# A 16 KB store of one row of 16 partitions, issued ahead of the first 4 MB store of a DMA-bound kernel

## Chip, cores and metric

One core of a Trainium2 chip. The metric is the device time of one execution in microseconds (us), the median over several executions. Each execution also has a span, the time from the first to the last recorded instruction of the core; the span of this kernel is about 1.6 us shorter than its device time. Fast means within 1.5% of the fastest execution of the same kernel. One core runs, so there is no die to compare.

## The reference

```python
W_adapted = W + scale * (lora_A @ lora_B)                 # 256 x 256
W_norm = np.sqrt(np.sum(W_adapted ** 2, axis=0, keepdims=True) + 1e-8)
W_final = W_adapted / W_norm * m
y = x.reshape(-1, 256) @ W_final                          # x: 16 x 2048 x 256, float32
```

x is 32 MB and y is 32 MB. The weights are small.

## The kernel before

The 32,768 rows are cut into 8 blocks of 4 MB. A block lies in SBUF as 128 partitions with one contiguous row of 32 KB each. There are 5 such buffers. SP issues the loads, and each result is written over its input in the same buffer, so a buffer is loaded, computed in place and stored. ACT copies the products out of PSUM, chunk by chunk (8 chunks of 512 KB per block), and issues the store when a block is complete. The last block is loaded and stored in two halves.

```python
def load_x(n):
    nc.sync.dma_start(
        out=in_sbuf(*parts[n]), in_=in_dram(x_flat, *parts[n])
    ).then_inc(sem(f"load{n}"), 16)

def store_y(n):
    nc.scalar.dma_start(
        out=in_dram(out_flat, *parts[n]), in_=in_sbuf(*parts[n])
    ).then_inc(sem(f"store{n}"), 16)

# ... SP: the first five loads at once, a later one when the store of its buffer has landed
for n in range(len(parts)):
    b = parts[n][0] // CH
    if b >= XBUFS and parts[n][0] % CH == 0:
        nc.sync.wait_ge(sem(f"store{b - XBUFS}"), 16)
    load_x(n)

# ... ACT
for g in range(NCH):                                   # 64 chunks
    b, c = divmod(g, CH)
    nc.scalar.wait_ge(sem("product"), g + 1)
    nc.scalar.copy(
        out=x_bufs[b % XBUFS][:, c * J : (c + 1) * J, :], in_=y_ps[g % 2][:]
    ).then_inc(sem("room"), 1)
    n = part_of[g]
    if g == NCH - 1 or part_of[g + 1] != n:
        nc.scalar.drain().then_inc(sem("done"), 1)
        nc.scalar.wait_ge(sem("done"), n + 1)
        store_y(n)
```

## Time and profile before

| | before |
|---|---|
| median of the timed executions | 163.63 us (163.5 to 163.79, 3 runs) |
| the execution that was profiled | 164.71 us, span 163.2 us |
| load queue q1 / store queue q10 | 49.0% / 47.8% of the 16 DMA engines' span |
| HBM traffic | 33.85 MB read, 33.55 MB written, 413 GB/s over the span |

Lines of the profile's page of the kernel before. The DMA and GB/s lines cut the span into 40 slices (4.08 us each): the first has the busy share of the DMA engines in tenths, the second what they moved. The q lines give packets, megabytes and the share of 16 engines' span.

```profile
span 163.2 us, 1988 instructions
...
DMA  5998998998999999999999999999999999998991
GB/s 201 402 498 386 426 474 385 482 418 265 466 426 426 442 410 466 426 394 482 418 426 442 420 426 458 402 458 410 446 414 454 414 446 422 450 442 377 442 430 60
...
q1 hardware_dynamic: 1440, 33.82, 49.0%
q10 hardware_dynamic: 1474, 33.59, 47.8%
```

The DMA engines are busy at eight tenths or more from the second slice to the last but one, so they bound the kernel. The tenth slice, with 265 GB/s, is the one low point on the way. (A slice holds only some 50 packets of 32 KB, so neighbours differ by some 100 GB/s without meaning.)

The timeline of the kernel before, ACT alone (start, duration, engine, line, operation; in brackets the idle time before it and what ended it):

```profile
23.65 1.93 ACT L219 COPY x_sb<-y_ps 128x1024 f32<-128x1024 f32 x2 [13.20 <-PE y_ps L281]
25.88 1.93 ACT L219 COPY x_sb<-y_ps 128x1024 f32<-128x1024 f32 x2 [0.30 <-PE y_ps L281]
30.26 1.93 ACT L219 COPY x_sb<-y_ps 128x1024 f32<-128x1024 f32 x2 [2.45 <-PE y_ps L281]
32.49 1.93 ACT L219 COPY x_sb<-y_ps 128x1024 f32<-128x1024 f32 x2 [0.30 <-PE y_ps L281]
34.52 0.37 ACTq L128 DMA_DIRECT2D out_dram<-x_sb  x1
```

The first store is issued at 34.52 us, right ahead of the low slice. The trace also holds every single DMA packet (start, duration, bytes, queue). A 32 KB row takes 1.213 us again and again. Between 36.1 and 38.4 us 25 load packets start that take 1.3 to 2.9 us. Adding up what those packets (the ones over 1.3 us) take beyond 1.213 us and dividing by 16 engines gives 1.29 us per engine. (The records do not name a packet's engine; "per engine" is here a sum over packets, or their number, divided by 16. In this trace 16 packets of 16 KB or more are on their way at once for 148 of the 163.2 us.) This sum is called "the stall" below. It is work on packet records, not a view of the profile. A count of bytes checks it: spreading the bytes of each packet evenly over its time, the core moved 413.7 GB/s from 20 to 50 us and 432.6 GB/s from 60 to 110 us, and what is missing in the first stretch is worth 1.3 us. So the stall is lost traffic and not only packets that overlap.

The packet records show a second loss. A store ends with 16 packets of 4 bytes. I take them as one for each engine, so that the last 16 of them tell when each engine was done: 15 engines have written their last byte by 160.3 us, one only at 162.7 us. 42 of the 896 store packets of 32 KB take 1.228 to 1.359 us (median 1.26), the others under that; no two of the 42 overlap by more than 0.01 us, so they fit one engine.

### The profile page before, as it was taken

Reading aid. Unit: us, or ns where it says so; the run is one execution under the profiler, and the core shown is the slowest. Engines: PE = TensorE matmul, PEld = TensorE weight load, DVE = VectorE, ACT = ScalarE, POOL = GpSimd, SP = SyncE. Lnnn points to the kernel's source line nnn. Section 1 sums busy time; section 2 is a strip of 40 time slices with the busy share of each in tenths; the row PEclk is TensorE's granted clock in tenths of the full one; section 3 lists DMA queues with packets and bytes.
Section 4 is the critical chain, followed back from the end, with each engine's and each line's share of the span. In section 5 each row is a group of like instructions: output and inputs, shape, how many; then the busy total and the mean of one; then the engine's idle time right before and its main releaser. Section 6 shows DMA issues by size and latency. Waiting matters only on the chain. (4 is left out here: it accounts for less than half of the span.)

```text
span 163.2 us, 1988 instructions
## 1 busy us (share of the span) xinstructions
PE 105.3 (65%) x786; PEld 85.2 (52%) x786; DVE 47.2 (29%) x44; ACT 63.8 (39%) x67; POOL 62.5 (38%) x39
## 2 busy tenths in 40 slices
PE   1270599789789897898981998619988820892000
PEld 0130577677577775776760867418676610771000
DVE  0429452350532514405230325005051400330000
ACT  3010027548366384473754053900738440062000
POOL 1006381753935738268004940069209003900000
PEclk9999999999999999999998589985899996599755
DMA  5998998998999999999999999999999999998991
GB/s 201 402 498 386 426 474 385 482 418 265 466 426 426 442 410 466 426 394 482 418 426 442 420 426 458 402 458 410 446 414 454 414 446 422 450 442 377 442 430 60
DMA packets 2915, 67.41 MB, mean 413 GB/s; under 512 B 465, under 2 KB 482, under 8 KB 610
## 3 DMA queue, kind: packets, MB, share of 16 engines
q1 hardware_dynamic: 1440, 33.82, 49.0%
q10 hardware_dynamic: 1474, 33.59, 47.8%
q14 instruction: 1, 0.01, 0.0%
HBM read 33.85 MB, written 33.55 MB: 413 GB/s over the span
## 5 line engine op out<-in xcount | busy, mean ns | idle before, releaser
L219 ACT COPY x_sb<-y_ps 128x1024 f32<-128x1024 f32 x64 | 61.9, 1014 | 75.8 <-PE y_ps L281 75.8
L165 POOL CAST xb<-x_sb 128x2048 bf16<-128x2048 f32 x32 | 60.0, 1902 | 79.3 <-DMA x_sb<-in_x_dram 56.0
L281 PE MATMUL y_ps<-w_final,xt 128*128 128x256 bf16 x512 | 64.6, 280 | 12.8 <-PEq L256 12.8
L202 DVE COPY xt<-xt_ps 128x1024 f32<-128x1024 f32 x32 | 38.2, 1221 | 88.1 <-PE xt_ps L267 88.0
L281 PEld LDWEIGHTS y_ps<-w_final,xt 128*128 128x128 bf16 x512 | 48.4, 100 | 28.2 <-issue 19.8
L267 PE MATMUL xt_ps<-identity,xb 128*128 128x128 f32 x264 | 39.1, 309 | 23.1 <-PEq L256 23.1
L267 PEld LDWEIGHTS xt_ps<-identity,xb 128*128 128x128 f32 x264 | 34.9, 161 | 25.8 <-issue 25.6
L198 DVE TENSOR_TENSOR w_final<-wam,rnorm 128x256 bf16<-128x256 f32 x2 | 4.0, 2028 | 0.0
L244 PE MATMUL y_ps<-sq,ones 128*128 128x256 f32 x4 | 2.1, 674 | 1.6 <-DVE sq L187 1.6
L233 PE MATMUL y_ps<-identity,a_nat 128*16 128x128 f32 x2 | 0.6, 397 | 3.6 <-DMA a_nat<-in_lora_A_dram 3.6
L212 ACT ACTIVATE norm<-y_ps,eps_col 128x256 f32<-128x256 f32 x1 | 0.5, 473 | 6.1 <-PE y_ps L244 6.1
L244 PEld LDWEIGHTS y_ps<-sq,ones 128*128 128x128 f32 x4 | 1.2, 323 | 2.3 <-DVE sq L187 2.1
L210 ACT ACT_TABLE_LOAD x1 | 1.3, 1283 | 2.4 <-issue 2.4
L233 PEld LDWEIGHTS y_ps<-identity,a_nat 128*16 128x16 f32 x2 | 0.1, 90 | 3.6 <-issue 3.6
L171 POOL MEMSET xb<- 128x2048 bf16 x1 | 1.8, 1805 | 0.3 <-PE xt_ps L267 0.3
L195 DVE RECIPROCAL rnorm<-norm 128x256 f32<-128x256 f32 x1 | 1.7, 1745 | 0.0
L237 PE MATMUL y_ps<-b_bf,aT 16*128 16x256 bf16 x2 | 0.6, 404 | 1.5 <-DVE aT L180 1.5
L189 DVE COPY m_all<-y_ps 128x256 f32<-128x256 f32 x1 | 0.4, 425 | 3.3 <-PE y_ps L249 3.3
L178 DVE CAST b_bf<-b_nat 16x256 bf16<-16x256 f32 x1 | 0.3, 281 | 3.8 <-DMA b_nat<-in_lora_B_dram 3.8
L249 PE MATMUL y_ps<-m_row,ones 1*128 1x256 f32 x2 | 1.2, 710 | 0.0
L237 PEld LDWEIGHTS y_ps<-b_bf,aT 16*128 16x128 bf16 x2 | 0.1, 106 | 1.9 <-DVE aT L180 1.9
L183 DVE SCALAR_TENSOR_TENSOR wa<-y_ps,w_nat 128x512 f32<-128x512 f32 x1 | 0.7, 692 | 0.8 <-PE y_ps L237 0.8
(13 smaller groups left out, 3.7 us busy)
## 6 DMA issues: line engine op xcount, KB each, us to landing
x_sb<-in_x_dram SPq DMA_DIRECT2D x7, 4096.0 KB, 27.1
out_dram<-x_sb ACTq DMA_DIRECT2D x7, 4096.0 KB, 37.2
x_sb<-in_x_dram SPq DMA_DIRECT2D x2, 2048.0 KB, 29.6
out_dram<-x_sb ACTq DMA_DIRECT2D x2, 2048.0 KB, 20.2
w_nat<-in_W_dram SPq DMA_DIRECT2D x1, 256.0 KB, 2.9
a_nat<-in_lora_A_dram ACTq DMA_DIRECT2D x1, 16.0 KB, 2.6
b_nat<-in_lora_B_dram ACTq DMA_DIRECT2D x1, 16.0 KB, 3.6
m_row<-in_m_dram ACTq DMA_DIRECT2D x1, 1.0 KB
```

What stands on the lines that cost most here:

```text
L165: nc.gpsimd.tensor_copy(out=xb_bufs[p % NXB][:], in_=x_bufs[b % XBUFS][:, 2 * c * J : 2 * (c + 1) * J, :],).then_inc(sem("rounded"), 1)
L171: nc.gpsimd.memset(xb_bufs[NPR % NXB][:], 0.0).then_inc(sem("rounded"), 1)
L183: nc.vector.scalar_tensor_tensor(out=wa[:], in0=ab_ps, scalar=float(scale), in1=w_nat[:], op0=ALU.mult, op1=ALU.add).then_inc(dv, 1)
L195: nc.vector.reciprocal(out=rnorm[:], in_=norm[:]).then_inc(dv, 1)
L198: i = nc.vector.tensor_mul(out=w_final[:, t], in0=wam[:, t], in1=rnorm[:])
L202: nc.vector.tensor_copy(out=xt_bufs[p % NXT][:].rearrange("p r t -> p (r t)").bitcast(FP32), in_=xt_ps[p % 2][:],).then_inc(sem("copied"), 1)
L210: nc.scalar.activation(out=warm[:], in_=eps_col[:], func=AF.Sqrt)
L219: nc.scalar.copy(out=x_bufs[b % XBUFS][:, c * J : (c + 1) * J, :], in_=y_ps[g % 2][:]).then_inc(sem("room"), 1)
L244: i = nc.tensor.matmul(n2_ps, ones[:], sq[:, t, :], start=(t == 0), stop=(t == KC - 1))
L249: nc.tensor.matmul(mb_ps, ones[0:1, :], m_row[:], start=True, stop=True).then_inc(pe, 1)
L267: i = nc.tensor.transpose(xt_ps[p % 2][:, j * P : (j + 1) * P], xb_bufs[p % NXB][:, j, :].bitcast(FP32), identity[:],)
L281: i = nc.tensor.matmul(y_ps[h][:, j, :], xt_bufs[p % NXT][:, r : r + P, t], w_final[:, t, :], start=(t == 0 and (j % (J // 2)) == 0), stop ...
```

## The change

The intent: let the first write of the program be a tiny one, so that whatever the first write costs does not hold up 32 KB rows of loads. After the second chunk, one row of 1 KB of each of 16 partitions goes out, meant as one packet for each DMA engine. The whole block is still stored later, over it.

```diff
         ).then_inc(sem("room"), 1)
+        if g == 1:
+
+            nc.scalar.drain().then_inc(sem("first"), 1)
+            nc.scalar.wait_ge(sem("first"), 1)
+            nc.scalar.dma_start(
+                out=in_dram(out_flat, *parts[0])[0:16, 0:1, :],
+                in_=x_bufs[0][0:16, 0:1, :],
+            ).then_inc(sem("ahead"), 16)
         n = part_of[g]
+        if n == 0 and g == NCH // NBLK - 1:
+            nc.scalar.wait_ge(sem("ahead"), 16)
         if g == NCH - 1 or part_of[g + 1] != n:
```

## The prediction

> **What bounds the kernel now.** The 16 DMA engines. The DMA part of the page has the load queue at 49.0% and the store queue at 47.8% of the engines' span, 158 of 163.2 us; the 40 slices show DMA at 9 nearly throughout. The other engines have room (PE 65%, ACT 39%). In the timeline a 4 MB block is computed in 13.2 us (first store issued at 34.52, second at 47.74), while its load and store take the DMA about 19.4 us. The chain of waits is no use: it covers 2% of the span. The last store is issued at 148.20 us; 15 us of store traffic follow. Time is won only where DMA engines now lose it.
>
> **What they lose.** In the records of single DMA packets a 32 KB row takes 1.213 us. One exception touches all 16 engines: from about 36 to 39.6 us, just after the first store is issued, load packets take 1.3 to 2.9 us. Summed and divided by 16, 1.3 us are lost per engine; the 40 slices show 265 GB/s in the tenth slice, where neighbours have 418 and 466. The first store packet starts 5 us after its issue. No later store brings this. I read it as a one-time cost of the first write to HBM, with loads stuck behind 16 rows of 32 KB.
>
> A second loss is not touched: one engine's store packets take about 1.26 us, and it finishes at 162.7 us, 2.4 us after the others.
>
> **What the change does.** It adds a store of 16 KB (16 partitions, 1 KB each) after the second copy out of PSUM, near 26 us, 9 us before the first whole store. Nothing is removed. Costs: a 1 KB packet takes 0.046 us, so 0.05 us per engine; ACT gives a drain, a wait and an issue of about 0.4 us, in a stretch where it idles 2.45 us before each four copies and where loads alone keep the DMA busy until about 48 us. If the whole store slips by 0.5 us, nothing waits for it. The added wait should be over before the eighth copy.
>
> The first write's cost should then fall on 1 KB per engine. [...] If instead the first write stops the memory for everybody, the 1.3 us move to 27 us.
>
> **Sum.** All avoided: 163.6 - 1.3 + 0.05 = 162.4. Merely moved: 163.7. I give avoidance, wholly or largely, 60%. What is saved counts in full, since DMA is busy to the end.
>
> Predicted 162.8 us, 8 in 10 between 161.9 and 163.9. Faster by over 2%: 0.02; within 2%: 0.96; slower: 0.02.
>
> **What would show it.** Right: the tenth slice over 400 GB/s, no packet over 1.5 us near 36 to 40 us, no slice below 380 near 26 to 31 us, the whole store's first packet within 3 us of its issue. Wrong (moved): an equal dip in the seventh or eighth slice. Wrong (cause is not the first write): the dip stays after the first whole store.
>
> **What would make it wrong.** The stall needs large rows or the first store's many descriptors rather than a first write; the small store completes so late that block 0's store slips by many us; the slow engine becomes slower or recovers (up to 2.4 us either way).

## The result, and the profile after

| | before | after |
|---|---|---|
| median | 163.69 us (163.5 to 163.79, 4 runs) | 163.68 us (163.62 to 163.72, 4 runs) |
| ratio after / before | | 1.000 (95% interval 0.9983 to 1.0017) |
| profiled execution | 164.71 us, span 163.2 | 163.72 us, span 162.1 |

A ratio is the mean time of one kernel's fast runs over that of the other's of the same rounds, so it is not quite the ratio of the medians.

The time did not change. The two profiles differ by 1.1 us in span, but the two profiled executions also differ by 1.0 us in device time. The first trace of the kernel before is therefore the wrong thing to compare with. Run e6 below profiled the unchanged kernel again, in an execution of 163.67 us; it is shown here with the changed kernel.

The page of the changed kernel, the same lines as shown of before, and its line on the new store (KB, us from issue to landing):

```profile
span 162.1 us, 1990 instructions
...
DMA  5999999998999999989999999999989999999992
GB/s 198 392 509 396 388 509 396 392 509 315 461 388 453 453 388 453 453 388 485 412 404 493 398 404 485 404 400 437 485 372 429 449 441 465 404 429 408 441 429 121
...
q1 hardware_dynamic: 1440, 33.82, 49.2%
q10 hardware_dynamic: 1506, 33.61, 48.2%
...
out_dram<-x_sb ACTq DMA_DIRECT2D x1, 16.0 KB, 6.4
```

The page of the unchanged kernel profiled again (run e6):

```profile
span 162.1 us, 1988 instructions
...
DMA  5999999997999999999999999999999999999993
GB/s 202 413 485 396 420 477 396 429 477 283 485 388 420 485 396 429 461 404 437 453 404 461 431 404 477 412 396 445 433 416 445 412 441 489 404 412 425 433 420 137
```

The span is the same to the tenth. The low tenth slice is still there after the change (315 GB/s against 283). The seventh and eighth slice, where the prediction put a moved stall (the small store's packets run in the eighth), are at 396 and 392 in the changed kernel and 396 and 429 in the unchanged one; the difference of 37 is within what neighbours differ by.

The timeline of the changed kernel, ACT alone:

```profile
23.45 1.93 ACT L219 COPY x_sb<-y_ps 128x1024 f32<-128x1024 f32 x2 [11.30 <-PE y_ps L291]
25.48 0.34 ACTq L226 DMA_DIRECT2D out_dram<-x_sb  x1
25.86 1.93 ACT L219 COPY x_sb<-y_ps 128x1024 f32<-128x1024 f32 x2 [0.49 <-PE y_ps L291]
30.06 1.93 ACT L219 COPY x_sb<-y_ps 128x1024 f32<-128x1024 f32 x2 [2.27 <-PE y_ps L291]
32.28 1.93 ACT L219 COPY x_sb<-y_ps 128x1024 f32<-128x1024 f32 x2 [0.30 <-PE y_ps L291]
34.32 0.37 ACTq L128 DMA_DIRECT2D out_dram<-x_sb  x1
```

The same stretch of e6 begins and ends with:

```profile
23.27 1.93 ACT L219 COPY x_sb<-y_ps 128x1024 f32<-128x1024 f32 x2 [12.58 <-PE y_ps L281]
...
34.14 0.37 ACTq L128 DMA_DIRECT2D out_dram<-x_sb  x1
```

The new store costs ACT 0.19 us (0.49 instead of 0.30 before the next pair of copies), and the next wait is shorter by 0.18 us. So issuing it is free.

From the packet records:

| | before, first profile | before again (e6) | after |
|---|---|---|---|
| device time of that execution | 164.71 | 163.67 | 163.72 |
| small store: packets start | | | 28.9 to 30.2 us |
| longest load packet starting from 26 to 31.5 us | 1.264 | 1.213 | 1.222 |
| whole store: issue, first packet | 34.52, 39.59 | 34.14, 39.26 | 34.32, 39.25 |
| stall at the whole store, us per engine | 1.29 | 0.96 | 0.71 |
| last byte of 15 engines / of the last engine | 160.3 / 162.7 | 160.1 / 161.6 | 160.2 / 161.6 |

The small writes pass among the loads without holding up any of them (no load packet over 1.222 us), and the whole store still stalls the loads. The count of bytes from 20 to 50 us agrees: against the same 432.6 GB/s, 0.9 us are missing in e6 (419.2 GB/s) and 0.7 us in the changed kernel (422.0). The longer first profile of before differs from e6 mostly by its slow engine: 1.1 us at its end, against 0.4 us for the mean of the other 15, which is about what its stall is longer (0.33 us).

### The profile page after: what moved, and what is told of

It is laid out like the page before. It is cut to its first block, busy times and chain, and to the rows that moved or that the text cites. A ratio compares the mean times of both kernels' runs of the same rounds, so it can differ in the third digit from the quotient of the medians.

```text
span 162.1 us, 1990 instructions
## 1 busy us (share of the span) xinstructions
PE 103.0 (64%) x786; PEld 83.7 (52%) x786; DVE 45.6 (28%) x44; ACT 63.6 (39%) x67; POOL 62.4 (38%) x39
## 5 line engine op out<-in xcount | busy, mean ns | idle before, releaser
L291 PE MATMUL y_ps<-w_final,xt 128*128 128x256 bf16 x512 | 63.4, 276 | 12.8 <-PEq L266 12.7
L291 PEld LDWEIGHTS y_ps<-w_final,xt 128*128 128x128 bf16 x512 | 47.8, 99 | 27.6 <-issue 19.6
L277 PE MATMUL xt_ps<-identity,xb 128*128 128x128 f32 x264 | 38.0, 303 | 23.8 <-PEq L266 23.8
L277 PEld LDWEIGHTS xt_ps<-identity,xb 128*128 128x128 f32 x264 | 34.0, 158 | 26.4 <-issue 26.2
L198 DVE TENSOR_TENSOR w_final<-wam,rnorm 128x256 bf16<-128x256 f32 x2 | 2.5, 1276 | 0.0
```

Source lines behind the costliest of these rows:

```text
L198: i = nc.vector.tensor_mul(out=w_final[:, t], in0=wam[:, t], in1=rnorm[:])
L277: i = nc.tensor.transpose(xt_ps[p % 2][:, j * P : (j + 1) * P], xb_bufs[p % NXB][:, j, :].bitcast(FP32), identity[:],)
L291: i = nc.tensor.matmul(y_ps[h][:, j, :], xt_bufs[p % NXT][:, r : r + P, t], w_final[:, t, :], start=(t == 0 and (j % (J // 2)) == 0), stop ...
```

## The experiments

Theory A: the stall does not belong to the first write. It comes when long store packets first run beside the loads, so a small store takes nothing away, and 0.71 against 0.96 is chance. Theory B: the small store does shrink the stall, and something else eats the gain. Rivals about the cause of the stall follow run by run. "Early" is always after the second chunk, as in the change.

### e1 and e6: the kernel before again; e2 and e5: the changed kernel again

No edit. e1 and e5 were the first kernel of their job.

> The kernel before, unchanged, profiled again, because the first profile of it came from an execution of 164.71 us while its timed runs have a median of 163.69. Theory A (the small store removed nothing, the two first profiles differ by chance): span about 162.1 us, stall of the loads at the first whole store about 0.7 us per engine, time ratio 1.000. Theory B (the small store halved the stall and something else ate the gain): span about 163.2 us with a stall of about 1.3 us again.

> The changed kernel, unchanged, profiled again. Theory A: time ratio 1.000 within 0.1%, and the stall at the first whole store between 0.7 and 1.3 us per engine, anywhere in the range that the kernel before shows. Theory B: stall again near 0.7 us, below that of the kernel before on this chip. Both: no stall when the small store's packets run near 29 us.

> The changed kernel as the first kernel of a job. Both profiles of the kernel before came from the first execution of a job (164.71 and 164.81 us, span 163.2), both of the changed kernel from later ones or other jobs (163.72 and 163.65, span 162.1). If it is the place in the job that costs 1.1 us, this profile shows a span near 163.2 us and its first time is near 164.7 us; the other times are 163.6 to 163.8. If the kernel before is slower under the profile by itself, this stays at 162.1.

> The kernel before, as the second kernel of a job, to have a trace of an execution as long as its timed ones. If the small store removed nothing: span 162.1 us, stall of the loads at the first whole store 0.7 to 0.9 us per engine as in the two traces of the changed kernel. If the small store does shrink it: 1.1 us or more at the same span.

| run | kernel | median, ratio to before (95%) | profiled execution | stall at the whole store |
|---|---|---|---|---|
| e1 | before | 163.61, 0.999 (0.998 to 1.000) | 164.81, span 163.2 | 1.06 |
| e6 | before | 163.66, 0.999 (0.997 to 1.001) | 163.67, span 162.1 | 0.96 |
| e2 | after | 163.73, 1.001 (0.9995 to 1.0025) | 163.65, span 162.1 | 0.84 |
| e5 | after | 163.85, 1.000 (0.997 to 1.003) | 163.90, span 162.4 | 0.94 |

e1 missed what theory A expected: its profiled execution was again a long one (its other six took 163.49 to 163.78), and its stall of 1.06 us lies between the two theories. Being first in the job is not enough for a long execution, as e5 shows. e1's trace does show where its extra time went. The loads stalled three times more, near 55, 75 and 94 us, by 0.39, 0.56 and 0.52 us per engine; the 16 engines ended 1.5 us later on average than in e6, and the last one 1.1 us later. Why these stalls come in some executions only is not shown. The page of e1 has the first stall in its ninth slice (257); of the later ones only those in slices 19 and 24 (361 and 363) stand out a little:

```profile
span 163.2 us, 1988 instructions
...
GB/s 201 426 474 385 490 410 393 506 257 474 418 426 458 385 401 458 418 434 361 450 434 434 450 363 434 426 458 385 434 458 401 438 434 422 482 409 418 414 434 173
```

e6 gave the trace that was wanted, and its 0.96 us too lies between what was expected if the small store removed nothing (0.7 to 0.9) and if it shrinks the stall (1.1 or more). With 0.71, 0.84 and 0.94 us after and 0.96 before at like times, the stall is not clearly different, and the ratio of the first comparison (0.9983 to 1.0017) allows at most about 0.3 us of gain or loss. Theory B is not excluded for a tenth or two of a microsecond. It is excluded as a halving: e5 has 0.94.

### e3: 128 partitions of 1 KB instead of 16

```diff
-                out=in_dram(out_flat, *parts[0])[0:16, 0:1, :],
-                in_=x_bufs[0][0:16, 0:1, :],
+                out=in_dram(out_flat, *parts[0])[:, 0:1, :],
+                in_=x_bufs[0][:, 0:1, :],
```

> The early store widened from 16 to 128 partitions, 1 KB each: 8 descriptors per engine and every 32 KB row of the block touched once. If the cost belongs to the first touch of each piece of the output or to the first long list of descriptors, the loads are held up near 29 us and the first whole store is free (under 0.2 us). If it belongs to the first long store packets (theory A's reading), nothing near 29 us, and 0.7 to 1.3 us at the whole store as before; time ratio 1.000 to 1.001 (128 KB more are 0.3 us of DMA).

Median 164.82 us, ratio 1.0065 (1.0051 to 1.0079). From 26 to 35 us, while its packets ran, no load packet was held up (0.00 us), and the whole store stalled the loads by 0.92 us. So neither the first touch of every 32 KB row of the block nor a list of 128 descriptors is what costs. The time is up by 1.1 us, more than expected. The profiled execution was its fastest (164.16 us, span 162.5), and its 8 packets of 0.046 us per engine account for 0.4 us; why the other five had spans of 163.2 to 163.5 us is open.

### e4: the first store in two pieces, nothing stored twice

```diff
-                out=in_dram(out_flat, *parts[0])[0:16, 0:1, :],
-                in_=x_bufs[0][0:16, 0:1, :],
+                out=in_dram(out_flat, *parts[0])[:, 0 : 2 * J, :],
+                in_=x_bufs[0][:, 0 : 2 * J, :],
...
+        j0 = 2 * J if n == 0 else 0
-            out=in_dram(out_flat, *parts[n]), in_=in_sbuf(*parts[n])
+            out=in_dram(out_flat, *parts[n])[:, j0:, :], in_=in_sbuf(*parts[n])[:, j0:, :]
```

> No byte is stored twice: block 0 is stored as 8 KB rows of all 128 partitions after the second chunk and as 24 KB rows after the eighth. If the cost comes when long packets of the store queue first meet the loads, the stall moves to about 29 us, perhaps smaller as the packets are a quarter (0.2 to 0.7 us per engine), and the later store of 24 KB rows, for which the queue is by then empty again, shows little or a stall of its own. If it is bound to the first write alone it is at 29 us in full (0.7 to 1.3 us) and nothing later. Time: 163.0 to 163.7 us.

Median 163.74 us, ratio 1.000 (0.9988 to 1.0012). Load packets were held up at three places: 0.29 us from 25 to 28, 0.11 near 33, and 0.17 near 44 us when the rows of 24 KB began, 0.57 us in all. So 8 KB packets, eight per engine, do meet the stall, in a milder form, where 1 KB packets do not. It lost less in all than the 0.96 us of e6, and no time was won. In its profiled execution the last engine ended at 161.5 us as ever.

### e7 and e10: a full 32 KB row per engine in the early store

Its data are the second block as loaded, written to rows that the whole store overwrites; the output is right. e7 takes partitions 0 to 15, e10 every eighth partition.

```diff
             nc.scalar.wait_ge(sem("first"), 1)
+            nc.scalar.wait_ge(sem("load1"), 16)
             nc.scalar.dma_start(
-                out=in_dram(out_flat, *parts[0])[0:16, 0:1, :],
-                in_=x_bufs[0][0:16, 0:1, :],
+                out=in_dram(out_flat, *parts[0])[0:128:8, :, :],     # e7: [0:16, :, :]
+                in_=x_bufs[1][0:128:8, :, :],                        # e7: [0:16, :, :]
```

> The early store of 16 partitions carries a full 32 KB row per engine instead of 1 KB (its data are the loaded second block, written to rows that the whole store overwrites, so the output is right). It adds 512 KB, 1.2 us per engine. If the stall belongs to the first long store packet of the program, 0.5 us or more move to 27 to 31 us and the whole store has under 0.2 us. If it is paid each time the store queue goes from empty to long packets while loads run, both places show it (0.3 us or more early, 0.5 us or more at the whole store). Time 164.8 to 165.5 us.

> The early store of 16 full 32 KB rows again, from every eighth partition instead of sixteen neighbours, because with neighbours the early packets themselves took 1.6 to 4.1 us. If that was crowding on the few SBUF partitions read, the packets now take 1.2 us, the loads near 27 us lose 0.5 to 1.0 us per engine, the whole store loses under 0.2, and the time is 164.6 to 165.3 us. If the early stall was not crowding, it stays at 1.5 us or more and the time at 166.7.

e7: 166.72 us, ratio 1.0158 (1.0111 to 1.0205), over the 165.5 us that were expected. Its 16 packets took 1.6 to 4.1 us each, 1.9 us per engine beyond 1.213, and the loads beside them lost 0.10 us. The whole store, whose packets begin at 37.05 us, stalled the loads by 0.01 us. e10: 164.69 us, ratio 1.0070 (1.0056 to 1.0085). Its 16 packets took 1.213 us each, the loads lost 0.60 us between 27.5 and 29 us, and the whole store 0.00.

The page of e10:

```profile
span 163.0 us, 1991 instructions
...
GB/s 197 414 482 394 418 482 386 386 418 482 386 458 442 386 474 426 402 482 402 434 458 394 452 442 394 482 410 450 386 434 462 450 386 446 458 386 434 426 430 133
```

The tenth slice is at 482 GB/s: no low point where the whole store begins. This is the result that fixes the place of the cost, and e7 agrees with it; each rests on one profiled execution. One long packet per engine beside the loads takes the stall over, though the store queue then moved no data for over 5 us (the last early packet ends at 32.2 us, the next starts at 37.75). It takes the stall over and does not remove it: 0.60 us are lost early instead, and the 512 KB add 1.2 us of traffic. Some of the 0.60 us may belong to the choice of partitions and not to the stall, since in e7, with neighbouring partitions, the loss at that place fell on the early packets themselves and was much larger; no run separates this.

### e8: the store queue made busy with a load

Kernel before, with the fifth load issued by ACT at the second chunk instead of by SP:

```diff
+        if g == 1:
+            nc.scalar.dma_start(
+                out=in_sbuf(*parts[4]), in_=in_dram(x_flat, *parts[4])
+            ).then_inc(sem("load4"), 16)
...
-        load_x(n)
+        if n != 4:
+            load_x(n)
```

> No early store. The fifth load is issued on the store queue, at the second chunk, so that this queue becomes busy with 32 KB packets that are loads; store 0 then follows behind it on a queue that is never empty. If the stall comes from a second queue becoming busy, it appears near 28 us with loads alone (0.5 us or more) and not at store 0. If it comes from writing to HBM, nothing near 28 us and 0.5 us or more when store 0's packets begin. Time 163.0 to 164.2 us.

Median 163.68 us, ratio 1.000 (0.997 to 1.002). The load's 32 KB packets ran on the store queue from 26.3 us, and none of its packets took over 1.225 us. The last packet of that load started at 43.5 us and the store's first at 46.3 us, so the queue did stand without data packets for a moment. Load packets of the other queue that started from 43.3 to 47.6 us lost 0.75 us, and another 0.28 us was lost near 77 us. A second queue becoming busy is not enough; the stall came with the store.

### e9 and e12: writing before the loads run

e9 writes 1 MB of zeros in 8 KB rows at the very start and holds the loads of x until it has landed. e12 stores one 32 KB row per engine after the first load and holds the second load until that has landed. Both drop the early store among loads; the whole store overwrites what they wrote. (Of each edit the wait of ACT for the early store ahead of store 0 is cut.)

```diff
+    nc.vector.memset(x_bufs[0][:, 0 : 2 * J, :], 0.0).then_inc(sem("blank"), 1)     # e9
+    nc.scalar.wait_ge(sem("blank"), 1)
+    nc.scalar.dma_start(
+        out=in_dram(out_flat, *parts[0])[:, 0 : 2 * J, :],
+        in_=x_bufs[0][:, 0 : 2 * J, :],
+    ).then_inc(sem("ahead"), 16)
+    nc.sync.wait_ge(sem("ahead"), 16)
...
```

```diff
+    load_x(0)                                                                       # e12
+    nc.scalar.wait_ge(sem("load0"), 16)
+    nc.scalar.dma_start(
+        out=in_dram(out_flat, *parts[0])[0:128:8, :, :],
+        in_=x_bufs[0][0:128:8, :, :],
+    ).then_inc(sem("ahead"), 16)
+    nc.sync.wait_ge(sem("ahead"), 16)
-    for n in range(len(parts)):
+    for n in range(1, len(parts)):
...
+        if g == 0:
+            nc.scalar.wait_ge(sem("ahead"), 16)
...
```

> No early store among loads. At the very start 1 MB of zeros (8 KB rows of 128 partitions) is written to the first block's rows, and the loads of x wait until it has landed; the whole store overwrites it. If the stall is a cost of the first bulk write of an execution, it is paid there, and the whole store of block 0 holds up the loads by under 0.2 us. If it comes from long stores meeting running loads for the first time, it stays at 0.7 to 0.95 us at the whole store. Time 167 to 171 us in both cases, because the loads start later.

> One 32 KB store packet per engine (every eighth partition) goes out after the first load has landed and before the second load is issued, so no load runs beside it. If what counts is that long store packets meet running loads, these packets take their 1.2 us and the whole store of block 0 still stalls the loads by 0.5 us or more. If the length of the first store packet alone counts, the whole store has under 0.2 us, and the cost shows as longer packets or not at all. Time 168 to 171 us, because the second load starts late.

e9: 169.10 us, ratio 1.0332 (1.0317 to 1.0347). Its early store packets of 8 KB took 0.307 to 0.341 us, a quarter of 1.213 us and a little: no start-up cost is seen in them. The whole store still stalled the loads by 0.77 us. e12: 170.60 us, ratio 1.0406 (1.0353 to 1.0458). Its 16 packets took 2.2 to 2.6 us with nothing beside them, about twice 1.213 us, and the whole store stalled the loads by 1.20 us. So e9's first write pays nothing that shows at its own place. e12's does take longer, though e10's packets from the same partitions took 1.213 us; why is not shown. What was written before the loads ran, short or long, does not spare the whole store the stall. The loads that start right behind these early stores lose 0.62 us (e9) and 0.65 us (e12) in their first packets as well, where the first loads of e6 lose 0.16 us. So the loss seems to go with stores and loads coming together, in either order; that is a reading, not a test. Both profiled executions were longer than the others of their kernel (e9 by 1.4 us, e12 by 0.4 us or more), and e9's shows three more stalls of 0.3 to 0.65 us at 60, 80 and 100 us, as e1's long execution has three of 0.4 to 0.6 us near 55, 75 and 94 us; so the stall is not strictly a matter of once.

### e13: one packet of 8 KB per engine

The changed kernel with `[0:128:8, 0 : 2 * J, :]` in place of `[0:16, 0:1, :]` on both sides.

> The changed kernel with 8 KB instead of 1 KB per engine in its early store, from every eighth partition: one descriptor per engine still, and as many bytes as the run with 128 rows of 1 KB, in one packet instead of eight. If packet length counts in proportion, 0.1 to 0.4 us per engine are lost near 28 us and what is left of 0.9 at the whole store. If only a full 32 KB packet pays it, nothing near 28 us and 0.7 to 0.95 at the whole store. Time ratio 1.000 to 1.003.

Median 163.98 us, ratio 1.0009 (0.997 to 1.005). The 16 packets ran at 30.0 to 30.4 us in 0.309 to 0.326 us and the loads lost nothing there; the whole store stalled them by 0.74 us.

The page of e13:

```profile
span 162.3 us, 1990 instructions
...
GB/s 198 392 509 396 396 509 388 420 436 339 484 420 388 509 396 388 501 404 388 501 404 412 486 388 436 460 392 436 412 448 440 408 436 501 412 388 440 436 408 145
```

The tenth slice is low again (339), where e10 with the same partitions and four times the bytes had 482. One short packet per engine, of 1 KB or of 8 KB, is not enough.

### e11: what decides the end

Kernel before, the last store cut into 120 and 8 partitions, each with a semaphore of its own:

```diff
-            store_y(n)
+            if n < len(parts) - 1:
+                store_y(n)
+            else:
+                for k, (p0, p1) in enumerate(((0, 120), (120, 128))):
+                    nc.scalar.dma_start(
+                        out=in_dram(out_flat, *parts[n])[p0:p1],
+                        in_=in_sbuf(*parts[n])[p0:p1],
+                    ).then_inc(sem(f"store{n + k}"), 16)
```

> Not about the stall, but about what decides the end: in every trace so far one engine's store packets take about 1.25 us and it ends 1.5 to 2.4 us after the other 15. Kernel before, the last store cut into 120 partitions and 8 partitions. [...] If that one is the slow engine, the last packets end about 1 to 1.6 us earlier and the ratio is 0.990 to 0.994. [...]

A miss: 167.04 us, ratio 1.0231 (1.0192 to 1.0270). ("That one" is an engine that the author took to have no part of the last 2 MB.) The trace shows a number alone: its last 39 packets of 4 bytes are 16 for the store before and 15 and 8 for these two. Which engines they are it does not show. The last store's rows of 16 KB, 0.611 us each before, took up to 2.5 us. It may be the choice of partitions, as it may in e7; that is a guess. From the start of the first to the end of the last of their 16 rows, e7 (neighbours) took 4.4 us, e10 and e12 (every eighth partition) 2.4 and 2.6 us. But no run separates this. Which engine is the slow one stays open. It does not stand out in every trace: in e12's all 16 engines end between 168.7 and 168.9 us.

Summary of the runs on the stall:

| early store, per engine | beside running loads | lost at its place | lost at the whole store |
|---|---|---|---|
| none (e6) | | | 0.96 |
| none, fifth load on the store queue (e8) | | | 0.75 |
| 1 x 1 KB (after, e2, e5) | yes | 0.00 | 0.71, 0.84, 0.94 |
| 8 x 1 KB (e3) | yes | 0.00 | 0.92 |
| 1 x 8 KB (e13) | yes | 0.00 | 0.74 |
| 8 x 8 KB (e4; rest in 24 KB rows) | yes | 0.40 | 0.17 |
| 1 x 32 KB (e10) | yes | 0.60 | 0.00 |
| 1 x 32 KB, 16 neighbours (e7) | yes | 0.10, and 1.9 in its own packets | 0.01 |
| 8 x 8 KB at the start (e9) | no | see text | 0.77 |
| 1 x 32 KB after load 0 (e12) | no | see text | 1.20 |

## Why the prediction was right or wrong

Point by point:

- **DMA bounds the kernel, the rest has room**: right. On the page of before DMA stays at 8 tenths or more from the second slice to the last but one, and PE is busy for 65% of the span, ACT for 39%. The issue of the small store moved ACT by 0.19 us and nothing followed from it.
- **The small store costs next to nothing**: right, 0.046 to 0.052 us per packet, and the added wait was over in time: it landed 6.4 us after its issue at 25.48 us, 2.4 us ahead of the whole store's issue. Of the 6.4 us, 3.4 passed before its first packet, behind queued loads of 32 KB rows; e9's 1 MB with no bulk load beside it landed in 3.9 us.
- **"I read it as a one-time cost of the first write to HBM"**, and from it **"The first write's cost should then fall on 1 KB per engine"**: wrong, and this is the step that failed. The changed kernel's first writes held up no load packet (longest 1.222 us), and the whole store stalled the loads as before (0.71 to 0.94 us against 0.96). In e9 a first write of 8 KB packets by itself showed no such cost (0.307 to 0.341 us a packet) and did not spare the whole store the stall (0.77 us); in e8 a second busy queue showed none (no packet of that load over 1.225 us); and with 8 KB per engine sent early beside running loads (e3, e13) the whole store still lost 0.92 and 0.74 us, with 32 KB (e10) 0.00, so in these runs somewhere between 8 KB and 32 KB per engine had to travel beside running loads before the stall was paid. Whether the length of a packet or the bytes in all decide it is open: e4's packets of 8 KB, eight per engine, paid a part (0.40 us, and 0.17 at the later store). The prediction named this among its own failures: "The stall needs large rows".
- **Avoid or move**: the prediction allowed for both, and gave avoidance 60%. e10 shows a move, with 0.60 us lost early for 0.96 at the whole store and 1.2 us of added traffic. No run removed the stall; e4 made it milder without a gain in time.
- **Its own tests**: the tenth slice was to rise over 400 GB/s, and was 315; the whole store's first packet was to come within 3 us of its issue, and came after 4.9 us; no dip was to appear where the small store runs, and none did. Of its three branches it is "cause is not the first write" that the trace shows.
- **The size, 1.3 us**: read from an execution 1.1 us longer than the timed ones. In one as long as those it was 0.96 us. The profiled execution's own time, 164.71 us, stood beside the median of 163.63, and the prediction does not mention it.
- **"What is saved counts in full"**: not shown. e4 lost some 0.4 us per engine less than e6; its engines ended 0.16 us earlier on average and the last one 0.07 us earlier, and its time ratio is 1.000 with 0.12% either way. The long execution of e1 had 1.6 us more of stalls than e6; its engines ended 1.5 us later on average, and it took 1.1 us longer. So stalls do reach the time, in these two traces not one for one. One slow engine ends 1.4 to 1.5 us after the other 15 in the traces of e6 and the changed kernel (2.4 us in the first trace of before), so a mean over 16 engines is not what decides the end.
- **"with loads stuck behind 16 rows of 32 KB"**: not what the records show as it stands: in e6 the stalled load packets start up to 3.5 us before the store's first packet, and 14 of the 31 have ended when it starts. The mechanism inside the engines stays open: why long stores beside running loads cost most of a microsecond the first time (0.71 to 1.06 us in before again, e1 and e6, and in the three traces of the changed kernel) and, in most of the profiled executions, hardly again.

The predicted 162.8 us was 0.9 us too low; the measured 163.68 us is the "merely moved" end of the sum (163.7), though for another reason: the stall was not moved, it was left where it was.

No version here beats the kernel before.

## What to carry to other kernels

Before a loss is sized from a trace, compare the profiled execution's time with the timed ones; a difference of the size of the expected gain can be the whole finding. An event that comes just after a first store may belong to that store's size or to its company rather than to its being first: vary bytes, place and company one at a time before building on the name. And where one of 16 DMA engines ends late (1.4 to 2.4 us here), a saving averaged over all of them need not show in the time.
